# Two layers of a hybrid diffusion backbone in float32: moving query, key and norm jobs within the emission order

## The chip, the cores and the metric

One Trainium2 chip, one of its cores. The metric is the device time of one execution in microseconds. Three executions of the kernel before took 2201.49, 2202.52 and 2205.49 us; the median, 2202.52 us, is the time to be compared with. All tensors are float32.

## The reference, cut to what matters

A stream `x` of 512 latent tokens and a prefix of 256 context tokens go through two layers of width 1024. In the second layer (`last`) the context gives keys and values alone.

```python
for l in range(DEPTH):
    hx = modulate(x, norm1_g[l], sh1, sc1)          # RMSNorm, scale, shift
    hc = modulate(xc, norm1_g[l], csh1, csc1)
    ux = hx @ w_in[l]                               # one wide input projection
    uc = hc @ (w_in[l][:, :KV_COLS] if last else w_in[l])
    kv_c = kv_heads(uc[..., :KV_COLS], ...)         # keys, values of mixers B, C, D
    kv_x = kv_heads(ux[..., :KV_COLS], ..., rope)
    q_x = query_heads(ux, ..., rope)                # queries; D's latent queries cq = rms_norm(...)
    br_x = latent_branches(...)                     # A pooling, B 2-D neighbourhood,
                                                    # C windowed with sinks, D latent attention
    mixed_x = merge_branches(br_x, gate_logits, w_branch[l], w_out[l])
    ...
    x = x + g1 * mixed_x
    x = x + g2 * swiglu(modulate(x, norm2_g[l], sh2, sc2), ...)
return rms_norm(x, final_norm_g)
```

`merge_branches` sums over the four mixers `sigmoid(gate logits) * (y @ w_branch)`; each of the four gates is a projection of the normed stream to 1024 channels.

## The kernel before

**Arithmetic.** Everything lies feature-major: 128 features on the partitions, tokens on the free axis (768 = 512 latent, `PL`, and 256 context, `PC`; the second layer's queries and gates have `PL` only). A float32 product is made of three matmuls of rounded halves: `hi*hi + lo*hi + hi*lo` (`mm3`, L149 to L151). Each weight tile is loaded raw by a DMA that SyncE issues (L163), ScalarE rounds it to `hi` (L143), GpSimd subtracts for `lo` (L157; VectorE does it, L146, in a few places). A weight slab of 1024 x 128 comes as two halves of 256 KB; there are three raw buffers and four `hi`/`lo` buffers.

**Order of the work.** The program is written by a hand-made order of jobs, `Stream`. A job is a generator that emits matmuls and yields after some of them the TensorE time that they are reckoned to need. When a job is taken from the queue, its weights and those of the next job in the queue are loaded (`step`). `defer(us, fn)` emits `fn` once that much reckoned time has been emitted; `need(key)` emits it at once; `until(job)` emits jobs until that one is done and (if `late`) flushes the deferred ones. `drive(attend(heads))` alternates pieces of attention with steps of the waiting jobs, so that these jobs' matmuls fill TensorE while VectorE and ScalarE make the softmax. After that, the framework's scheduler lays each engine's instructions in a row, by priority of emission but with its own estimates of what is ready; only SyncE's order, that of the loads, is kept as written:

```python
ctx.enter_context(tc.manual_schedule(engines={SP}))
```

**PSUM.** Tags `mm` (3 banks, projections), `sc` (2, scores and the norm's `nh`), `tr` (2, transposes), `pv` (1). Scratch tiles of tag `t` (seven) hold rope halves, `tmv`, `krt`, `krx`, `braw` and others.

**Start of the second layer** (`mix`, L1325 to L1338). The pooling job runs (`ps_pool`), then the first neighbourhood queries (`ps_naq`), while the context's norm is finished: `norm.stats(PC)` and, 2.0 us of reckoned time later, `norm.apply(PC)` (L491 `ps_rstd`, L518 `nh`, L520 `hh`, L521 `hl`). Then come the token-major rows, `tm_jobs`: eight jobs with six accumulators (`ps_tm`), whose values are copied out (`tmv`, L665), stored to DRAM (`vst`, L667) and loaded back as values (`vraw`, L693 ff.). Then the first keys, `na_k_job(0)` (`ps_nak`, split by `split_k` into `k` tiles, L143, L146, L958), then attention B. `na_q_job(1)` (`ps_naq` again, weights `naqr`) and four gates of mixer A are the jobs that attention B is interleaved with. `na_bias` loads `braw` (L1004) and GpSimd adds the mask (L1011); these tables are needed by the first softmax (L1028).

**Mixer C in either layer** (L1358 to L1367). The keys job `swk` and the second queries job `swq` (both with rope: `rt` L143, then `rf` and `rt`, L1069, L1072, L1073, then the splits) run first; then attention C, interleaved with two `cq` jobs (the latent queries of D, with squares, statistics and a normalisation, `rms_jobs`) and six gates of mixer B. In attention, `sc` (L921, L922) are score matmuls, `mx` (L1108, L1110) maxima, `nm` their negative, `p` (L1114, L1115) the exponentials, normalised at L839, `tr` (L858) transposes, `pv` (L872) products with values.

**Norm behind a projection** (`project_jobs`). After each output tile `m` the residual `x` is made (`add_x`, L1458) and the tile's squares are deferred by 1.5 us (L1462; ScalarE L472 `nsq`, VectorE L473 `acc`). When the last of eight tiles is done, `stats` (L480 `ps_ssq`, then the small Newton steps `nwv`, `nwt`, then `dg`, L484) is deferred by 2.0 us and `apply` by 5.5 us.

Of the kernel before, what the change touches and what calls it, by code (L numbers as in the profile page):

```python
# [23 lines left out]
KD = D // 128  # L24
# [90 lines left out]
def kernel(ctx: ExitStack, tc: tile.TileContext, a: dict, out: bass.AP):  # L115
# [90 lines left out]
    def feat_job(w, c0, name, pieces, post):  # L206

        def run(ws):
            for p in pieces:
                ps = psum("mm", "ps_" + name, p[1] - p[0])  # L210
                yield from mm_piece(ps, ws, cur["h"], p)
                post(ps, p)
        return st.add(run, lambda: slab(w, c0, name))
# [413 lines left out]
    for l in range(2):  # L627
# [352 lines left out]
        def na_q_job(pr):  # L980
            q = []

            def post(ps, piece):
                if not q:
                    q.extend(new_q())
                split_q(ps, piece, q, True)
            return feat_job(w_in, O_NA_Q + 128 * pr, "naq", pieces, post), q

        def na_k_job(pr):
            k = []  # L990

            def post(ps, piece):
                if not k:
                    k.extend(new_k(4))
                split_k(ps, piece, k[0:2], k[2:4], True)
            return feat_job(w_in, O_NA_K + 128 * pr, "nak", (PL, PC), post), k
# [81 lines left out]
        def swa_q_job(g, tab):  # L1078
            q = []

            def post(src, piece):
                if not q:
                    q.extend(new_q())
                split_q(src, piece, q, False)
            return rope_job(O_SWA_Q + 128 * g, "swq", pieces, tab, post), q

        def swa_k_job(tab):
            k = []

            def post(src, piece):  # L1090
                if not k:
                    k.extend(new_k(4))
                split_k(src, piece, k[0:2], k[2:4], False)
            return rope_job(O_SWA_K, "swk", (PL, PC), tab, post), k
# [80 lines left out]
                    yield (s1 - s0) / 1200  # L1175
            return st.add(run)

        def rms_jobs(c0, dst, pieces_, name):

            box, acc_ = [], {}  # L1180

            def keep(i, ps, piece):
                if not box:
                    box.extend(dst())
                s0, s1 = piece
                n = s1 - s0
                hi, lo = (t[:, s0:s1] for t in box[i])
                act_copy(hi, ps)
                sub_hi(lo, ps, hi)
                if i == 0:  # L1190
                    acc_[piece] = tmp([128, n], F32, "nacc")
                acc = acc_[piece]
                square_add(acc, ps, i == 0)
                if i < len(box) - 1:
                    return

                def stats():
                    dg = rstd_diag(acc, n, 1.0 / (128 * len(box)))

                    def rest():  # L1200
                        rstd = rstd_rows(dg, n)
                        for j, b in enumerate(box):
                            hi, lo = (t[:, s0:s1] for t in b)
                            f = tmp([128, n], F32, "cf")
                            nc.vector.tensor_tensor(out=f, in0=hi.bitcast(F32), in1=lo.bitcast(F32), op=ALU.add)
                            nc.vector.scalar_tensor_tensor(out=f, in0=f, scalar=c_rms(l, len(box), j), in1=rstd, op0=ALU.mult, op1=ALU.mult)
                            act_copy(hi, f)
                            sub_hi(lo, f, hi)
                    st.defer(2.5, rest)
                st.defer(2.0, stats)  # L1210

            jobs = [feat_job(w_in, c0 + 128 * i, name, pieces_, lambda ps, p, i=i: keep(i, ps, p)) for i in range((1, 2)[name == "cq"])]
            return jobs[-1], box

        def mla_q_job(pr, tab, cq):
            qs = []
# [82 lines left out]
        def mix():  # L1299
            nam = big("c", [128, 3, 32, 8], F32, "nam")  # L1300
            nc.sync.dma_start(nam, a["k_namask"])
            y_pool = []
            bias, v = [], []

            def after_tm():
                v.extend((na_v(0, 4.0), na_v(1, 20.0)))
                rope_keys()
                cur["lo"] = nc.gpsimd

            if not last:  # L1310
                cur["lo"] = nc.vector

                tm = tm_jobs()
                for k in range(4):
                    ada_run((10, 10, 0, 0)[k])
                    st.until(tm[k], False)
                for k in range(4, KD):
                    start_h(k)
                jobs = pool_jobs(y_pool)
                jq0, q0 = na_q_job(0)  # L1320
                jk, k0 = na_k_job(0)
                st.until(tm[-1], False)
                after_tm()
                st.until(jobs[1], False)
            else:  # L1325
                jobs = pool_jobs(y_pool)
                jq0, q0 = na_q_job(0)
                norm.stats(PC)
                st.defer(2.0, lambda: norm.apply(PC), "norm")
                st.until(jobs[0], False)  # L1330
                st.need("norm")
                tm = tm_jobs()
                jk, k0 = na_k_job(0)
                st.until(tm[-1], False)
                after_tm()
            jq1, q1 = na_q_job(1)
            bias = [na_bias(e, nam) for e in range(2)]
            st.until(jk, False)  # L1338
            v0, v1 = v
            st.defer(24.0, lambda: bias.extend(na_bias(2 + e, nam) for e in range(2)), "bias")  # L1340
            y_na = [pair("y", TQ, "yn") for _ in range(2)]
            for m in range(4):
                g = gate_job(0, y_pool, m)
            st.drive(attend(na_heads(0, k0, q0, v0, bias[0:2], y_na[0])))
            jk, k1 = na_k_job(1)
            tab = [big("c", [128, 512], F32, "tab") for _ in range(2)]
            for i in range(2):
                nc.sync.dma_start(tab[i], a["k_rope"][:, i, :])
            vs = swa_v()
            g = gate_job(0, y_pool, 4)  # L1350
            st.until(g)
            st.need("bias")
            _, qs0 = swa_q_job(0, tab)
            jc, ck = rms_jobs(O_CKV, lambda: [pair("c", NT, "ck")], (PL, PC), "ckv")
            for m in range(5, KD):
                g = gate_job(0, y_pool, m)
            st.drive(attend(na_heads(1, k1, q1, v1, bias[2:4], y_na[1])))
            st.until(g)  # L1358
            jk, ks = swa_k_job(tab)
            jq, qs1 = swa_q_job(1, tab)  # L1360
            jc, cq = rms_jobs(O_CQ, lambda: [pair("c", TQ, "cq") for _ in range(2)], pieces, "cq")
            st.until(jq)
            y_swa = [pair("y", TQ, "ys") for _ in range(2)]
            for m in range(6):
                gate_job(1, y_na, m)
            heads = [h for g, q in enumerate((qs0, qs1)) for h in swa_heads(g, ks[g], ks[2 + g], q, vs, y_swa[g])]
            st.drive(attend(heads))  # L1367
            kt, vm = [], []
            rope_rows_job(kt)
            mtab = big("c", [128, 512], F32, "mtab")  # L1370
            nc.sync.dma_start(mtab, a["k_mrope"])
            mla_v_job(ck[0], vm)
            gate_job(1, y_na, 6)
            mla_k_job(0, ck[0], kt)
            _, qm = mla_q_job(0, mtab, cq)
            st.until(gate_job(1, y_na, 7))
            y_mla = [pair("y", TQ, "ym") for _ in range(2)]
            for m in range(4):
                gate_job(2, y_swa, m)
            st.drive(attend(mla_heads(qm, kt, vm[0:2], y_mla[0])))  # L1380
            mla_k_job(1, ck[0], kt)
            _, qm = mla_q_job(1, mtab, cq)
            st.until(gate_job(2, y_swa, 4))
            for m in range(5, KD):
                gate_job(2, y_swa, m)
            st.drive(attend(mla_heads(qm, kt, vm[2:4], y_mla[1])))
            return y_mla
# [61 lines left out]
        def project_jobs(w, name, h_, b, new_norm, first, rest, r0=0, kn=KD):  # L1449
# [4 lines left out]
            def add_x(ps, m, p):  # L1454
                s0, s1 = p
                c = 0 if s0 < NX else 1
                x = cur["x"][m][:, s0:s1]
                nc.vector.scalar_tensor_tensor(out=x, in0=ps, scalar=mods[l][:, b + m, c:c + 1], in1=x, op0=ALU.mult, op1=ALU.add)  # L1458
                if new_norm:
                    if not nm:  # L1460
                        nm[0] = new_norm()
                    st.defer(1.5, lambda: nm[0].squares(m, p), p)  # L1462

            def go(m, w_, ps_, tag="mm"):
                for p in ps_:
# [314 lines left out]
```

## Time and profile before

| | us |
|---|---|
| three executions | 2201.49, 2202.52, 2205.49 |
| the profiled execution, its own time | 2200.1 |
| its span, first to last instruction | 2198.3 |
| TensorE (PE) busy | 2131.2 (97% of the span) |
| VectorE (DVE) busy | 1261.2 (57%) |
| ScalarE (ACT) busy | 884.1 (40%) |
| GpSimd (POOL) busy | 732.7 (33%) |

The profiled execution took 2.42 us less than the median; 1.8 us of its 2200.1 lie outside the span. Busy times overlap; an engine's busy time is that of its instructions, without register, branch and semaphore work. A row of the timeline has the start in us from the span's start, the duration, the engine, the source line, the operation, what it writes and reads, the shape and, in brackets, the engine's idle time before it with what ended it. `SPq` and `ACTq` rows are the issuing of DMAs.

### The profile page before, as it was taken

Reading aid. Unit: us, or ns where it says so; the run is one execution under the profiler, and the core shown is the slowest. Engines: PE = TensorE matmul, PEld = TensorE weight load, DVE = VectorE, ACT = ScalarE, POOL = GpSimd, SP = SyncE. Lnnn points to the kernel's source line nnn. Section 1 sums busy time; section 2 is a strip of 40 time slices with the busy share of each in tenths; the row PEclk is TensorE's granted clock in tenths of the full one; section 3 lists DMA queues with packets and bytes.
Section 4 is the critical chain, followed back from the end, with each engine's and each line's share of the span. In section 5 each row is a group of like instructions: output and inputs, shape, how many; then the busy total and the mean of one; then the engine's idle time right before and its main releaser. Section 6 shows DMA issues by size and latency. Waiting matters only on the chain.

```text
span 2198.3 us, 32640 instructions
## 1 busy us (share of the span) xinstructions
PE 2131.2 (97%) x11840; PEld 1830.5 (83%) x11840; DVE 1261.2 (57%) x2818; ACT 884.1 (40%) x1981; POOL 732.7 (33%) x609
## 2 busy tenths in 40 slices
PE   6989999999999999999999999999999999999998
PEld 2878888888888888888888888887888898888886
DVE  6674667767789797554522255667777445212225
ACT  4364555544432322122212234556655434323233
POOL 1432222222232323323333333433333343444443
PEclk9999999999999999999999999999999999999999
DMA  7422121111455244444422232322222332333332
GB/s 239 114 61 62 48 51 44 39 49 49 127 175 151 85 150 133 143 140 149 151 75 63 70 111 83 103 66 66 56 65 70 88 115 82 96 96 97 103 93 91
DMA packets 317334, 211.59 MB, mean 96 GB/s; under 512 B 17371, under 2 KB 284917, under 8 KB 317173
## 3 DMA queue, kind: packets, MB, share of 16 engines
q1 hardware_dynamic: 308756, 201.65, 31.9%
q10 hardware_dynamic: 8416, 7.87, 1.1%
q8 instruction: 93, 1.52, 0.3%
q14 instruction: 69, 0.56, 0.1%
HBM read 202.90 MB, written 6.55 MB: 95 GB/s over the span
## 4 chain that ended last, share of the span: by engine, by line
PE 84%; DVE 6%; DMA 2%; ACT 2%; issue 2%; POOL 1%; ACTq 0%; SPq 0%; POOLq 0%; DVEq 0%
PE ps_w L149 13%; PE ps_w L150 13%; PE ps_w L151 13%; PE ps_gate L149 6%; PE ps_gate L150 6%; PE ps_gate L151 6%; PE pv L872 3%; PE tr L858 2%; PE ps_y L149 2%; PE ps_y L151 1%; PE ps_y L150 1%; PE ps_wo L151 1%; PE ps_wo L150 1%; PE ps_wo L149 1%; DMA wor<-in_w_out_dram 1%
## 5 line engine op out<-in xcount | busy, mean ns | idle before, releaser
L157 POOL TENSOR_TENSOR gatelo<-gater,gatehi 128x512 fp32r<-128x512 f32 x128 | 172.0, 1346 | 427.8 <-ACT gatehi L143 413.9
L149 PE MATMUL ps_gate<-hh,gatehi 128*128 128x512 f32 (+1 forms) x768 | 278.5, 363 | 1.2 <-ACT gt L807 1.2
L150 PE MATMUL ps_gate<-hl,gatehi 128*128 128x512 f32 (+1 forms) x768 | 273.5, 356 | 0.0
L151 PE MATMUL ps_gate<-hh,gatelo 128*128 128x512 f32 (+1 forms) x768 | 273.1, 356 | 0.0
L400 DVE SCALAR_TENSOR_TENSOR adaacc<-adaraw,cs,adaacc 128x512 f32<-128x512 f32 x224 | 160.8, 750 | 86.4 <-DMA adaraw<-in_ada_w_dram 85.1
L149 PE MATMUL ps_w<-hh,w1hi 128*128 128x512 f32 (+1 forms) x480 | 170.9, 356 | 0.0
L149 PE MATMUL ps_w<-hh,w3hi 128*128 128x512 f32 (+1 forms) x480 | 170.3, 355 | 0.0
L150 PE MATMUL ps_w<-hl,w1hi 128*128 128x512 f32 (+1 forms) x480 | 170.0, 354 | 0.0
L150 PE MATMUL ps_w<-hl,w3hi 128*128 128x512 f32 (+1 forms) x480 | 170.0, 354 | 0.0
L157 POOL TENSOR_TENSOR w1lo<-w1r,w1hi 128x512 fp32r<-128x512 f32 x80 | 103.6, 1296 | 198.9 <-ACT w1hi L143 196.9
L151 PE MATMUL ps_w<-hh,w1lo 128*128 128x512 f32 (+1 forms) x480 | 169.8, 354 | 0.0
L151 PE MATMUL ps_w<-hh,w3lo 128*128 128x512 f32 (+1 forms) x480 | 169.8, 354 | 0.0
L149 PE MATMUL ps_w<-gh,w2hi 128*128 128x512 f32 (+1 forms) x472 | 165.6, 351 | 0.0
L151 PE MATMUL ps_w<-gh,w2lo 128*128 128x512 f32 (+1 forms) x472 | 165.4, 350 | 0.0
L150 PE MATMUL ps_w<-gl,w2hi 128*128 128x512 f32 (+1 forms) x472 | 165.2, 350 | 0.0
L157 POOL TENSOR_TENSOR w3lo<-w3r,w3hi 128x512 fp32r<-128x512 f32 x80 | 105.5, 1325 | 178.1 <-ACT w3hi L143 170.3
L151 PEld LDWEIGHTS ps_gate<-hh,gatelo 128*128 128x128 f32 x768 | 145.1, 189 | 19.8
L149 PEld LDWEIGHTS ps_gate<-hh,gatehi 128*128 128x128 f32 x768 | 145.3, 189 | 19.0 <-ACT gt L807 1.4
L150 PEld LDWEIGHTS ps_gate<-hl,gatehi 128*128 128x128 f32 x768 | 145.4, 189 | 16.8
L157 POOL TENSOR_TENSOR w2lo<-w2r,w2hi 128x512 fp32r<-128x512 f32 (+1 forms) x80 | 97.4, 1224 | 158.2 <-ACT w2hi L143 156.9
L1515 DVE SCALAR_TENSOR_TENSOR ft<-ft,ps_w 128x512 f32<-128x512 f32 (+1 forms) x68 | 39.6, 582 | 143.9 <-ACT ft L1514 143.8
L143 ACT ACTIVATE gatehi<-gater 128x512 fp32r<-128x512 f32 x128 | 80.4, 630 | 83.4 <-PE ps_gate L150 41.9
(421 smaller groups left out, 5621.0 us busy)
## 6 DMA issues: line engine op xcount, KB each, us to landing
adaraw<-in_ada_w_dram SPq DMA_DIRECT2D x160, 256.0 KB
gater<-in_w_in_dram SPq DMA_DIRECT2D x128, 256.0 KB
w1r<-in_ffn_w_dram SPq DMA_DIRECT2D x80, 256.0 KB
w3r<-in_ffn_w_dram SPq DMA_DIRECT2D x80, 256.0 KB
w2r<-in_ffn_w_dram SPq DMA_DIRECT2D x56, 256.0 KB
ada<-in_ada_w_dram SPq DMA_DIRECT2D x32, 256.0 KB
wbr<-in_w_branch_dram SPq DMA_DIRECT2D x64, 128.0 KB
wor<-in_w_out_dram SPq DMA_DIRECT2D x32, 256.0 KB
```

Of the source, the lines that this page charges most:

```text
L143: nc.scalar.activation(out=o, in_=i, func=AF.Copy, scale=scale)
L149: nc.tensor.matmul(ps, ah, bh, start=start, stop=False)
L150: nc.tensor.matmul(ps, ah, bl, start=False, stop=False)
L151: return nc.tensor.matmul(ps, al, bh, start=False, stop=stop).ins
L157: cur["lo"].tensor_tensor(out=lo, in0=raw, in1=hi.bitcast(F32), op=ALU.subtract)
L400: nc.vector.scalar_tensor_tensor(out=acc[j], in0=raw, scalar=c, in1=acc[j], op0=ALU.mult, op1=ALU.add)
L858: nc.tensor.transpose(tr[:, 128 * j:128 * j + 128], ps[qi][0][:, c0:c0 + 128], ident)
L872: nc.tensor.matmul(acc[:, 128 * q0:128 * (q0 + nq)], v[rows], t[rows, c:c + 128 * nq], start=(i == 0), stop=(i == nmm - 1))
L1515: nc.vector.scalar_tensor_tensor(out=t, in0=t, scalar=1.0, in1=p1, op0=ALU.add, op1=ALU.mult)
```

## The change

Three edits. In mixer C, only the keys job precedes attention; the second queries and the two `cq` jobs follow in the queue, each with a gate before it: gate 0, `swq`, gate 1, `cq` 0, gate 2, `cq` 1, gates 3 to 5. In `add_x`, the last tile's squares are emitted at once, after any of the same piece that are still deferred. In the second layer, the job of the first keys stands ahead of the token-major rows, and `norm.apply(PC)` is deferred by 4.0 instead of 2.0 us.

```diff
-        def rms_jobs(c0, dst, pieces_, name):
+        def rms_jobs(c0, dst, pieces_, name, between=lambda i: None):
...
-            jobs = [feat_job(w_in, c0 + 128 * i, name, pieces_, lambda ps, p, i=i: keep(i, ps, p)) for i in range((1, 2)[name == "cq"])]
-            return jobs[-1], box
+            for i in range((1, 2)[name == "cq"]):
+                between(i)
+                job = feat_job(w_in, c0 + 128 * i, name, pieces_, lambda ps, p, i=i: keep(i, ps, p))
+            return job, box
...
                 jobs = pool_jobs(y_pool)
                 jq0, q0 = na_q_job(0)
+                jk, k0 = na_k_job(0)
                 norm.stats(PC)
-                st.defer(2.0, lambda: norm.apply(PC), "norm")
+                st.defer(4.0, lambda: norm.apply(PC), "norm")
                 st.until(jobs[0], False)
                 st.need("norm")
                 tm = tm_jobs()
-                jk, k0 = na_k_job(0)
                 st.until(tm[-1], False)
                 after_tm()
             jq1, q1 = na_q_job(1)
...
             jk, ks = swa_k_job(tab)
+            st.until(jk)
+            y_swa = [pair("y", TQ, "ys") for _ in range(2)]
+            gate_job(1, y_na, 0)
             jq, qs1 = swa_q_job(1, tab)
-            jc, cq = rms_jobs(O_CQ, lambda: [pair("c", TQ, "cq") for _ in range(2)], pieces, "cq")
-            st.until(jq)
-            y_swa = [pair("y", TQ, "ys") for _ in range(2)]
-            for m in range(6):
+            jc, cq = rms_jobs(O_CQ, lambda: [pair("c", TQ, "cq") for _ in range(2)], pieces, "cq", lambda i: gate_job(1, y_na, 1 + i))
+            for m in range(3, 6):
                 gate_job(1, y_na, m)
...
-                    st.defer(1.5, lambda: nm[0].squares(m, p), p)
+                    if m < KD - 1:
+                        st.defer(1.5, lambda: nm[0].squares(m, p), p)
+                    else:
+                        st.need(p)
+                        nm[0].squares(m, p)
```

## Rows read from the trace of the kernel before

**Rows 1.** The page: busy us of each engine, share of the span, instructions.
```profile
PE 2131.2 (97%) x11840; PEld 1830.5 (83%) x11840; DVE 1261.2 (57%) x2818; ACT 884.1 (40%) x1981; POOL 732.7 (33%) x609
```
**Rows 2.** PE's timeline in mixer C, rows with a wait (first, then second layer).
```profile
306.35 0.38 PE L921 MATMUL sc<-k,q 128*128 128x256 f32 x1 [1.90 <-DVE mx L1108]
...
339.41 0.70 PE L491 MATMUL ps_rstd<-dg,ones 128*128 128x256 f32 x2 [1.02 <-DVE dg L484]
...
1505.15 0.38 PE L921 MATMUL sc<-k,q 128*128 128x256 f32 x1 [1.13 <-ACT p L1114]
...
1511.79 0.39 PE L921 MATMUL sc<-k,q 128*128 128x256 f32 x1 [2.36 <-DVE mx L1108]
...
1532.77 0.30 PE L858 MATMUL tr<-ident,p 128*128 128x128 f32 x1 [0.69 <-DVE pl L146]
```
**Rows 3.** Timeline around the second layer's keys of mixer C: PE, DVE, POOL.
```profile
1494.70 0.28 PE L151 MATMUL ps_swk<-hh,swklo 128*128 128x256 f32 x1
...
1495.28 3.44 POOL L157 TENSOR_TENSOR cqlo<-cqr,cqhi 128x512 fp32r<-128x512 f32 x2 [8.12 <-ACT cqhi L143]
...
1495.90 1.66 DVE L1073 TENSOR_TENSOR rf<-rf,rt 128x512 f32<-128x512 f32 x1
...
1499.62 0.42 DVE L958 CAST k<-k 64x512 fp32r<-64x512 f32 x1
...
1506.00 0.68 DVE L1073 TENSOR_TENSOR rf<-rf,rt 128x512 f32<-128x512 f32 x1
```
**Rows 4.** Timeline at the first layer's last `wo` tile: squares, statistics, norm.
```profile
737.01 0.75 DVE L1458 SCALAR_TENSOR_TENSOR x<-ps_wo,mod,x 128x512 f32<-128x512 f32 x1 [3.48 <-PE ps_wo L151]
737.79 0.63 ACT L472 ACTIVATE nsq<-x 128x512 f32<-128x512 f32 x1 [4.99 <-DVE x L1458]
...
738.46 0.69 DVE L473 TENSOR_TENSOR acc<-acc,nsq 128x512 f32<-128x512 f32 x1 [0.70 <-ACT nsq L472]
...
739.68 0.95 PE L480 MATMUL ps_ssq<-ones,acc 128*128 128x2 f32 x8
```
**Rows 5.** PE's timeline at the second layer's start, rows that matter.
```profile
1327.11 0.70 PE L491 MATMUL ps_rstd<-dg,ones 128*128 128x256 f32 x2 [0.92 <-DVE pb L727]
...
1337.21 0.46 PE L149 MATMUL ps_tm<-tmhi,hh 128*128 128x416 f32 x1 [1.23 <-DVE hl L521]
...
1358.94 0.39 PE L149 MATMUL ps_nak<-hh,nakhi 128*128 128x512 f32 x1
...
1367.30 0.25 PE L921 MATMUL sc<-k,q 128*128 128x192 f32 x1
...
1370.02 0.50 PE L151 MATMUL ps_naq<-hh,naqlo 128*128 128x512 f32 x1 [0.81 <-POOL naqlo L157]
...
1378.16 0.33 PE L858 MATMUL tr<-ident,p 128*128 128x128 f32 x1 [1.75 <-DVE p L839]
...
1380.30 0.52 PE L858 MATMUL tr<-ident,p 128*128 128x128 f32 x3 [0.88 <-DVE p L839]
```
**Rows 6.** The loads and weight splits there: SyncE's issues, ACT, POOL.
```profile
1360.23 1.98 SPq L1004 DMA_DIRECT2D braw<-in_k_rpb_dram  x2
1363.93 2.44 SPq L163 DMA_DIRECT2D naqr<-in_w_in_dram  x2
...
1367.81 0.63 ACT L143 ACTIVATE naqhi<-naqr 128x512 fp32r<-128x512 f32 x1 [0.33 <-DMA naqr<-in_w_in_dram]
...
1368.52 1.45 POOL L157 TENSOR_TENSOR naqlo<-naqr,naqhi 128x512 fp32r<-128x512 f32 x1 [0.32 <-ACT naqhi L143]
1370.59 1.30 POOL L157 TENSOR_TENSOR naqlo<-naqr,naqhi 128x512 fp32r<-128x512 f32 x1 [0.62 <-DMA gater<-in_w_in_dram]
```
**Rows 7.** SyncE's own waits, 1320 to 1400 us: total us, times, longest us.
```profile
SPq L1004 <- DMA vst<-tmv: 9.4, 2, 8.6
```
**Rows 8.** PE's timeline where it stood longest after the start-up.
```profile
124.98 0.56 PE L149 MATMUL ps_pw<-yph,pwh 128*128 128x256 f32 x1 [4.69 <-DVE ypl L766]
```
**Rows 9.** Stretch behind that: us, busy PE, PEld, DVE, ACT, POOL, PEclk, DMA, GB/s.
```profile
125.10:128.40 3.30, 3.22 (x10) 2.31 (x11) 3.03 (x6) 3.18 (x8) 2.68 (x2) 0.50 0.18 36
```

## The prediction

> **What bounds the kernel now.** I read the page's busy times first [rows 1]: TensorE (PE) is busy for 97% of the span, VectorE for 57%. The change adds and removes no matmul, so the time can move only through the moments in which PE stands. Next I took PE's waits by releaser, and then its timeline at the places that the change touches. There the reader is to look at the brackets: how long PE stood, and for whom.
>
> In mixer C it stands five times that matter [rows 2]: 1.90 us in the first layer and 1.13 and 2.36 us in the second, all in the first 17 us of attention C and for the softmax; later 1.02 us for the statistics of the latent queries and 0.69 us for a transposed tile. At the second layer's start it stands 0.92 us for the context's norm, 1.23 us for its last halves, 0.81 us for weights, and 1.75 and 0.88 us for the first softmax [rows 5]. That is 7.10 + 5.59 = 12.69 us, 0.6% of the time: at these places no more can be won.
>
> **Part 1, last squares at once: 0.** This edit changes priority alone. In the trace the deferred squares are not late: the residual ends at 737.76, ScalarE squares it from 737.79, VectorE has added it by 739.15, and the statistics' matmuls start at 739.68 [rows 4]. They stand behind two steps of other matmuls in the program (2.0 us of deferral), which the edit leaves alone. The three norms that have such a tile show the same pattern. What hides the squares is an idle ScalarE; without that, one square and one addition (0.63 + 0.69 us) would wait. I take 0, with 0.5 us either way.
>
> **Part 2, mixer C: -2.6.** Moved are the `swq` job (24 matmuls a piece, two weight loads, four copies on ScalarE, three rope steps and the splits on VectorE), the two `cq` jobs with their two loads each, and three gates with three loads each. SyncE has the gate's three loads ahead of `swq`'s; all find their buffers as the old ones did, since each job takes two of the same four halves. GpSimd has the same number of differences in another order.
>
> What goes: the three early waits, 1.90 + 1.13 + 2.36 = 5.39 us, in which the softmax stood behind the rope of `swq`, now two jobs later. What stays: 1.02 + 0.69, whose chains are only moved. What is new: the keys were covered by `swq`. The last key matmul starts at 1494.70 and the last copy of the first head's keys ends at 1500.04 [rows 3], 5.2 us later once that matmul is through. The gate that now follows in the queue is ready and would fill PE, if the framework's scheduler puts it ahead of the scores; it does order by its estimates: ScalarE had rounded `cqhi` by 1495.28, ahead of its copies of the older keys, whose rope was not added until 1495.90 [rows 3]. If the scores stand first, every gate matmul waits behind them on PE, and the softmax with them. So the wait is between 0 and 5.2 us in either layer. It hangs on how far the scheduler's estimate is off, and the rope's last addition took 1.66 us beside GpSimd's `cqlo` and 0.68 us at another moment [rows 3]: about 1 us of surprise. I take 0.7 us in either layer, 1.4, nearest to that row.
>
> The Trainium skill (SBUF — State Buffer, section "Who interferes with whom") says that a VectorE instruction with two inputs in SBUF and a GpSimd one that reads SBUF shut each other out for a whole instruction. By that rule the longer of the two durations holds wherever a weight split falls on the keys, and without it the sum would be 1.4 us lower; the 1.66 us agree with the rule.
>
> The moved rope also meets a running softmax later; I take the same 0.7 us for it in each layer, 1.4. Sum: -5.39 + 1.4 + 1.4 = -2.6 us. Bounds: -7.1 (all five waits go, none comes) and +5.0 (the scores wait 5.2 us in both layers: 10.4 - 5.4).
>
> **Part 3, the first keys ahead of the rows: +4.1.** Moved are 48 matmuls, two loads and the splits of the keys. They ran from 1358.94 to 1367.30 [rows 5], 8.36 us, which is 36 matmuls of 512 columns at 0.232 us. In that time something else went on. SyncE waited up to 8.6 us for the stores of the rows before it could load the bias tables [rows 7], at 1360.23; the second queries' weights stand behind these in its queue, with the first gates' behind them, and were issued from 1363.93 on [rows 6]. ScalarE rounded the first half at 1367.81, GpSimd was through with it at 1368.52 + 1.45 = 1369.97 and with the second at 1371.89. PE, with 8.36 us of keys to do, still stood 0.81 us for them.
>
> This order of loads is unchanged, since SyncE's is kept as written and `na_q_job(1)` is loaded only when `drive` takes it. Counted from the end of the rows, the halves arrive at +11.03 and +12.95 us. Before, the keys and 10.86 us of other things lay between the rows and the first transposes (1378.16 - 1367.30); of these 0.81 + 1.75 were waits, 8.30 work. After the change PE has about 1.2 us of scores, then nothing until the first half is there; 10 matmuls take it to 13.35, 12 more to 16.1, and up to 1.2 us of scores and transposes to 17.3. Against 10.86 that is 5.2 to 6.4 us later; I take 6.0, since waits rarely pack. Off go the 0.88 us of the second transposes, whose softmax starts earlier now, and 1.0 of the norm's 0.92 + 1.23: the keys give the context's norm 5 us more, but their own accumulators hold banks that the rows need. Sum: 6.0 - 0.9 - 1.0 = +4.1 us. Bounds: -5.6 (all five waits go, none comes) and +8.1 (6.4 us and nothing saved, and 1.7 us of half clock, below).
>
> **Sum.** 0 - 2.6 + 4.1 = +1.5 us on the profiled execution's 2200.1, so 2201.6; that execution lies 2.4 us under the median, so 2204.0 us is to be compared with 2202.52. A measurement of this kernel can tell 0.2%, 4.4 us, from no change.
>
> **Rivals.**
>
> *Rival 1, slower: the gap also costs the clock.* After the longest stand, 4.69 us [rows 8], TensorE was granted 0.50 of its clock (1.2 of 2.4 GHz) from 125.1 to 128.4 us [rows 9]: 3.3 us of work done in half, 1.7 us lost. A gap of 8 us at the second layer's start would be followed by the same, so part 3 costs 6.4 + 1.7 = 8.1 us with no norm wait saved; with part 2 at -2.6 that is +5.5, 2208.0. It decides as soon as part 3 costs over 7.0. For it: the load order; against: the matmuls that follow wait for a second half anyway, so half a clock hides there. On the page TensorE: Matmul & The Clock Gate (section "What's actually happening") the Trainium skill calls the half rate the default that activity lifts; by that rule this gap is followed by it, and rows 8 and 9 agree.
>
> *Rival 2, faster: the weights are not late.* If the store that SyncE waits for lands sooner, or the scheduler keeps some of the rows' matmuls for the gap, part 3 is at its lower bound: -5.6 - 2.6 = -8.2, 2194.3. For it: the loads' issue has only 1.3 us after the rows to wait for stores [rows 5, 6]. Against: all of the chain behind it is measured, and 36 matmuls of cover are gone.
>
> *Rival 3, part 2 does nothing.* The scheduler orders by its own estimates already, and waits only change place: 0 + 4.1, 2206.6, inside 0.2%. For it: the same estimates made the old waits; against: the rope itself leaves the busiest stretch.
>
> **How the numbers follow.** Forecast 0.42, rival 1 0.30, rival 2 0.20, rival 3 0.08. The forecast's own spread puts 0.02 of it beyond 0.2% on each side. Faster is then 0.20 + 0.02 = 0.22, slower 0.30 + 0.02 = 0.32, same 0.38 + 0.08 = 0.46. As cases of both signs hold half of the chance, the forecast's own range is 2200 to 2207.5. The range of 8 in 10 goes from 2196.5 to 2210.5: it leaves out half of rival 2 (0.10) and the upper end of rival 1, with part 2 near its upper bound (0.08).
>
> **What would show it.** Part 1 is right if `ps_ssq` follows its last square as before and no wait of a norm goes. Part 2 is right if no wait over 1 us stands in the first 17 us of attention C, and a new one of under 1.5 us stands at the first scores. Part 3 is right if, after the last `ps_tm`, PE stands some 8 us in all for `naqhi` and `naqlo`, with `braw` still ahead of them on SyncE, and no longer stands for the first softmax. It is wrong if these weights are ready within 3 us of the rows' end; the sum is wrong too if waits arise away from these places, since the scheduler lays the whole program anew.

## The result and the profile after

The kernel after takes 2217.22 us (median of six executions, 2211.88 to 2220.01); the kernel before took 2203.17 beside it (six executions, 2200.33 to 2205.49). The ratio is 1.0065, with a 95% interval of 1.0051 to 1.0079: slower by 14 us, where +1.5 was forecast and 2210.5 was the upper end of the range. The profiled execution of the kernel after is one of its longer ones (2218.24 us, span 2216.4), that of the kernel before one of its shorter ones, so between the spans of these two traces 18.1 us are to be found.

The page's first part, to be held against [rows 1]:

```profile
PE 2138.9 (97%) x11840; PEld 1834.3 (83%) x11840; DVE 1260.0 (57%) x2818; ACT 884.4 (40%) x1981; POOL 730.7 (33%) x609
```

The work is the same, instruction for instruction. PE's busy time is 7.7 us longer for the same 11840 matmuls, and the rest of the 18.1 us is standing. To find where, I cut both traces at the same PE instructions. The views below have a row for each of three stretches: from the first layer's last key matmul of mixer C to its first `wo` matmul; from the last pooling matmul to the second layer's first key matmul of mixer C; from its last key matmul to its first `wo` matmul. The columns are those of [rows 9], with the stretch's length after its bounds. First the kernel before:

```profile
290.88:679.25 388.37, 380.74 (x2349) 336.05 (x2347) 300.70 (x709) 191.55 (x503) 94.98 (x83) 1.00 0.29 81
1322.63:1486.51 163.88, 156.72 (x829) 134.38 (x828) 98.21 (x276) 89.53 (x206) 61.71 (x56) 1.00 0.32 86
1494.70:1767.75 273.05, 265.36 (x1369) 218.31 (x1368) 186.65 (x440) 151.80 (x386) 96.42 (x85) 1.00 0.28 72
```

Then the kernel after:

```profile
291.04:690.07 399.03, 385.72 (x2349) 338.52 (x2348) 300.29 (x709) 192.35 (x502) 94.18 (x82) 0.99 0.28 78
1334.13:1502.77 168.64, 158.87 (x829) 135.90 (x828) 97.45 (x276) 88.41 (x207) 61.05 (x57) 0.97 0.31 83
1510.96:1787.46 276.50, 266.59 (x1370) 219.24 (x1369) 185.10 (x440) 151.88 (x385) 95.42 (x84) 0.99 0.27 70
```

The lengths differ by +10.66, +4.76 and +3.45 us, 18.87 in all; the other stretches give 0.8 back. So the first layer's mixer C, where no loss was expected, holds more than half. PE's timeline there, rows with large brackets that the kernel before does not have:

```profile
295.28 0.50 PE L921 MATMUL sc<-k,q 128*128 128x256 f32 x2 [1.21 <-ACT k L143]
...
299.26 0.44 PE L921 MATMUL sc<-k,q 128*128 128x384 f32 x1 [0.62 <-DVE mx L1108]
...
306.93 0.85 PE L858 MATMUL tr<-ident,p 128*128 128x128 f32 x6 [0.83 <-DVE nm L831]
...
330.55 0.90 PE L858 MATMUL tr<-ident,p 128*128 128x128 f32 x3 [1.64 <-DVE p L839]
...
377.07 1.05 PE L480 MATMUL ps_ssq<-ones,nacc 128*128 128x2 f32 x8 [2.87 <-DVE nacc L473]
...
396.59 0.38 PE L921 MATMUL sc<-k,q 128*128 128x256 f32 x1 [0.67 <-DVE cf L1206]
...
451.30 0.47 PE L149 MATMUL ps_uq<-cqh,wqhi 128*128 128x512 f32 x1 [1.72 <-DVE qt L1233]
```

In the first 17 us of attention C stands what was forecast: no 1.90 us wait of the softmax any more, and a new one of 1.21 us at the first scores. The loss lies behind it: 1.64 us for a normalised tile, 2.87 us for the latent queries' sum of squares, and 1.72 us in mixer D, where 1.23 us stood at a neighbouring matmul before (`wqlo`, 436.00). Behind the first two of these the granted clock is half. The same view by stretches, of the kernel after, with the second layer's start and mixer D's start in the second layer as third and fourth row:

```profile
330.50:333.90 3.40, 3.35 (x10) 2.66 (x11) 2.26 (x7) 1.75 (x5) 0.00 (x0) 0.50 0.00 0
378.30:381.70 3.40, 3.40 (x11) 2.72 (x10) 2.88 (x16) 2.00 (x7) 0.00 (x0) 0.50 0.20 68
1381.80:1392.00 10.20, 5.20 (x11) 3.68 (x12) 5.09 (x14) 3.50 (x11) 8.06 (x9) 0.50 0.65 176
1634.40:1637.80 3.40, 3.40 (x10) 2.62 (x9) 1.99 (x6) 1.24 (x4) 0.99 (x1) 0.50 0.30 77
```

Taking half of PE's busy time in such a stretch as lost, an estimate from these rows gives 1.7, 1.7, 2.6 and 1.7 us. (One and the same place, shown in the last section, has 21 matmuls in 3.40 us at the full clock and 11 at half.) At the second layer's start, the loads, the rounding and PE, to be held against [rows 5, 6]:

```profile
1377.70 0.35 PE L151 MATMUL ps_tm<-tmhi,hl 128*128 128x416 f32 x1
...
1379.22 1.42 SPq L1004 DMA_DIRECT2D braw<-in_k_rpb_dram  x2
1380.74 1.27 SPq L163 DMA_DIRECT2D naqr<-in_w_in_dram  x2
...
1385.29 0.63 ACT L143 ACTIVATE naqhi<-naqr 128x512 fp32r<-128x512 f32 x1 [5.76 <-POOL bias L1011]
...
1385.97 0.80 PE L149 MATMUL ps_naq<-hh,naqhi 128*128 128x512 f32 x1 [6.59 <-ACT naqhi L143]
...
1388.03 0.80 PE L151 MATMUL ps_naq<-hh,naqlo 128*128 128x512 f32 x1 [0.83 <-POOL naqlo L157]
```

`braw` is still ahead of `naqr` on SyncE, and PE stands 7.42 us for the two halves. (The row of `naqhi` names GpSimd's bias tables; in the kernel with all parts and both repairs the same row names the load, `[5.99 <-DMA naqr<-in_w_in_dram]`.) SyncE itself waited up to 14.1 us for the rows' stores ahead of `braw`, where [rows 7] have 8.6 (here from 1340 to 1410 us):

```profile
SPq L1004 <- DMA vst<-tmv: 14.4, 2, 14.1
```

In the second layer's mixer C the two waits of [rows 2] are gone and others have come, the longest far behind, at the scores of mixer D:

```profile
1515.20 0.50 PE L921 MATMUL sc<-k,q 128*128 128x256 f32 x2 [1.21 <-ACT k L143]
...
1632.74 0.50 PE L149 MATMUL sc<-k,q 96*128 96x512 f32 x1 [2.76 <-ACT p L1283]
```

### The profile page after: what moved, and what is told of

It reads as the page before. It is cut to its first block, busy times and chain, and to the rows that moved or that the text cites. A ratio compares the mean times of both kernels' runs of the same rounds, so it can differ in the third digit from the quotient of the medians.

```text
span 2216.4 us, 32641 instructions
## 1 busy us (share of the span) xinstructions
PE 2138.9 (97%) x11840; PEld 1834.3 (83%) x11840; DVE 1260.0 (57%) x2818; ACT 884.4 (40%) x1981; POOL 730.7 (33%) x609
## 5 line engine op out<-in xcount | busy, mean ns | idle before, releaser
L157 POOL TENSOR_TENSOR w3lo<-w3r,w3hi 128x512 fp32r<-128x512 f32 x80 | 105.1, 1320 | 179.1 <-ACT w3hi L143 177.6
L149 PEld LDWEIGHTS ps_gate<-hh,gatehi 128*128 128x128 f32 x768 | 145.9, 190 | 19.2 <-ACT gt L807 1.4
```

What stands on the lines that cost most here:

```text
L149: nc.tensor.matmul(ps, ah, bh, start=start, stop=False)
L157: cur["lo"].tensor_tensor(out=lo, in0=raw, in1=hi.bitcast(F32), op=ALU.subtract)
```

## The experiments

**The parts one by one.** The first three kernels are the kernel before with one part of the change each; their diffs are parts of the one shown above (the edit in `add_x`; those in `rms_jobs` and mixer C; the one in the second layer's start).

> Part 1 alone: the last tile's squares at once, all else as before. Theory (the loss of 14 us sits in mixer C of the first layer, and part 1 is worth nothing): within 2 us of the kernel before, and the statistics' matmuls of the norms start as in rows 4. Rival A (the framework's scheduler lays the whole program anew at any edit, and this alone moves the time): 5 us or more away in either direction, with waits at places that no edit touches.

Measured: 2200.87 us against 2201.79, ratio 1.0004 (0.9996 to 1.0013). The theory's figure holds. In its trace the last square starts at 738.75 and the statistics' matmuls at 740.64, 1.89 us apart as in [rows 4].

> Part 2 alone: in mixer C only the keys precede attention, the second queries and the latent queries stand between gates, in both layers. Theory (the normalisation of the latent queries now meets a running softmax on VectorE, and the waits that follow lower the granted clock): +8 to +14 us, with the 2.87 us wait for the latent queries' sum of squares and the stretches at 0.50 of the clock in the first layer's mixer C, as in the trace of the kernel after. Rival A (part 2 is worth its forecast, the 14 us come from part 3 and from where its waits fall in the clock): -5 to +2 us. Rival B (the parts are not additive: either alone is harmless): within 2 us.

Measured: 2211.95 us against 2201.79, ratio 1.0053 (1.0039 to 1.0066), some 12 us. The theory holds: 2.88 us for the sum of squares and half clock are there again.

> Part 3 alone: the second layer's first keys precede its token-major rows, the context's norm is deferred by 4.0 instead of 2.0 us. Theory (the second queries' weights come late, behind the bias tables on SyncE): +3 to +7 us, with some 7 us of standing for the two halves of these weights and a stretch at 0.50 of the clock behind it. Rival A (most of the 14 us is here): +10 us or more. Rival C (the weights are late only after part 2's delay): -5 to 0 us.

Measured: 2206.02 us, ratio 1.0024 (1.0015 to 1.0034), some 5 us. PE stands 6.69 and 0.84 us for the two halves, and 0.50 of the clock stands behind it. The three parts add up: 0.0004 + 0.0053 + 0.0024 = 0.0081, against 0.0065 for the whole; the intervals overlap.

**Part 3 with its loads in order.** Part 3 alone, with this edit on top:

```diff
                 tm = tm_jobs()
+                jq1, q1 = na_q_job(1)
                 st.until(tm[-1], False)
                 after_tm()
-            jq1, q1 = na_q_job(1)
+            if not last:
+                jq1, q1 = na_q_job(1)
```

> Part 3 with its load order mended: in the second layer the job of the second queries is queued right behind the rows' jobs, so that SyncE issues its weights ahead of the stores' wait and the bias tables. Theory (the loss of part 3 is this load order alone): the 7 us of standing for the weights go, no stretch at half clock at the second layer's start, and the time is 0 to 6 us below the kernel before. Rival D (the gap stays, and only its name changes, since attention B's first softmax waits for the bias tables in the same queue, which are then later by two loads): +2 to +7 us, with PE standing for the first transposes instead.

Measured: 2204.48 us, ratio 1.0016 (1.0005 to 1.0027). My theory falls, rival D's figure holds. SyncE now issues `naqr` at 1355.82 and PE no longer stands for it, but the next weights in the same queue, and then the values, which ScalarE loads, are late instead. PE's timeline:

```profile
1378.65 0.50 PE L149 MATMUL ps_gate<-hh,gatehi 128*128 128x512 f32 x1 [2.20 <-ACT gatehi L143]
...
1381.00 0.50 PE L151 MATMUL ps_gate<-hh,gatelo 128*128 128x512 f32 x1 [1.16 <-POOL gatelo L157]
...
1391.53 0.39 PE L872 MATMUL pv<-ph,v 128*128 128x256 f32 x1 [1.60 <-DVE v L146]
```

So it is not the place of one pair of loads alone. It fits these rows that the keys' 8.36 us were the cover for all that is stored and loaded between the rows and attention B, since the gates and the values now come late one after the other; no run tests this by itself. Whether anything is gained over part 3 alone (1.0024) the intervals cannot tell.

**Part 2 taken apart.** From the kernel before; the first diff is mixer C with only the second queries moved, the second with only the latent queries taken apart (both with `between` in `rms_jobs` where it is used).

```diff
+            st.until(jk)
+            y_swa = [pair("y", TQ, "ys") for _ in range(2)]
+            gate_job(1, y_na, 0)
             jq, qs1 = swa_q_job(1, tab)
             jc, cq = rms_jobs(O_CQ, lambda: [pair("c", TQ, "cq") for _ in range(2)], pieces, "cq")
-            st.until(jq)
-            y_swa = [pair("y", TQ, "ys") for _ in range(2)]
-            for m in range(6):
+            for m in range(1, 6):
```

> From the kernel before: in mixer C of both layers only the second queries move (keys, attention begins, gate 0, second queries); the two latent-query jobs stay unbroken behind them, then gates 1 to 5. Theory (the loss of part 2 is the latent queries' sum of squares, which now stands among gates whose weights GpSimd splits; the second queries' move costs little): -2 to +4 us. Rival A (the moved rope of the second queries and the keys' lost cover are the loss): +7 to +12 us, the same as part 2 alone.

Measured: 2207.08 us against 2202.26, ratio 1.0024 (1.0014 to 1.0034), 5 us: between the theory's figure and the rival's. The 1.64 us wait at the normalised tile is here too, behind the second queries' rope and splits on VectorE. Its VectorE and PE rows:

```profile
322.63 1.58 DVE L1073 TENSOR_TENSOR rf<-rf,rt 128x512 f32<-128x512 f32 x1
...
324.92 1.71 DVE L971 SCALAR_TENSOR_TENSOR q<-rf,q 64x512 fp32r<-64x512 f32 x2
...
327.42 0.15 DVE L831 TENSOR_SCALAR nm<-mx 128x1 f32<-128x1 f32 x1
...
330.70 0.48 DVE L839 TENSOR_SCALAR p<-p,rs 128x512 f32<-128x512 f32 x1
...
331.24 0.72 PE L858 MATMUL tr<-ident,p 128*128 128x128 f32 x3 [1.64 <-DVE p L839]
```

```diff
             jq, qs1 = swa_q_job(1, tab)
-            jc, cq = rms_jobs(O_CQ, lambda: [pair("c", TQ, "cq") for _ in range(2)], pieces, "cq")
             st.until(jq)
             y_swa = [pair("y", TQ, "ys") for _ in range(2)]
-            for m in range(6):
+            jc, cq = rms_jobs(O_CQ, lambda: [pair("c", TQ, "cq") for _ in range(2)], pieces, "cq", lambda i: gate_job(1, y_na, i))
+            for m in range(2, 6):
```

> From the kernel before: the second queries stay ahead of attention C, only the latent queries are taken apart (gate 0, latent 0, gate 1, latent 1, gates 2 to 5). Theory (the latent queries' chain among the gates is the loss): +4 to +9 us, with a wait of some 3 us for their sum of squares and half clock behind it in the first layer. Rival A (the second queries' move is the loss): -2 to +2 us.

Measured: 2205.28 us, ratio 1.0012 (1.0000 to 1.0024), 2.6 us, between the two figures; the interval reaches both. The theory's wait does not come: taken apart by themselves, the latent queries show no wait for the sum of squares. The waits of [rows 2] for the maxima are still there (1.89 and 2.33 us), since the second queries are still in front. By the middles of the ratios the two halves of part 2 cost 8 us by themselves and 12 together, so some of the loss may be what they do to each other; the intervals are too wide to settle that.

Next, part 2 in the first layer alone (`if not last:` around the new lines, the old ones behind `else:`).

> Part 2 in the first layer alone. Theory (in the trace the first layer's mixer C holds +9.5 us and the second layer's +2 to +3): +7 to +11 us. Rival (the layers share the loss, and the profiled execution was not typical): +4 to +6 us.

Measured: 2211.43 us, ratio 1.0038 (1.0024 to 1.0051), 8 us. The theory's figure holds, though the interval (5.3 to 11.2 us) touches the rival's.

**The sum of squares.** Around the wait of 2.87 us the kernel after shows, on GpSimd and VectorE:

```profile
373.62 2.85 POOL L157 TENSOR_TENSOR gatelo<-gater,gatehi 128x512 fp32r<-128x512 f32 x2 [6.56 <-ACT gatehi L143]
...
373.85 1.50 DVE L146 TENSOR_TENSOR ysl<-yf,ysh 128x256 fp32r<-128x256 f32 x1
...
375.27 1.74 DVE L473 TENSOR_TENSOR nacc<-nacc,nsq 128x512 f32<-128x512 f32 x1
```

The addition `nacc` took 0.68 us in the kernel before. The view of this tile has minimum, median and maximum of its three additions in ns, in the kernel before and then after:

```profile
L473 DVE TENSOR_TENSOR nacc<-nacc,nsq x3: 416/676/691, 322.6 to 1520.9; 128x512 f32<-128x512 f32 x2, 128x256 f32<-128x256 f32 x1
```

```profile
L473 DVE TENSOR_TENSOR nacc<-nacc,nsq x3: 416/691/1744, 375.3 to 1568.3; 128x512 f32<-128x512 f32 x2, 128x256 f32<-128x256 f32 x1
```

Both VectorE instructions have two inputs in SBUF, and each ends a little after one of GpSimd's two splits (the second at 373.62 + 2.85 = 376.47, `nacc` at 375.27 + 1.74 = 377.01). This agrees with the rule of the Trainium skill (SBUF — State Buffer, section "Who interferes with whom") that the prediction weighed for the keys alone. The addition alone takes 0.69 us and the copy 0.42 us (medians of the kernel after), so the two are some 2.1 us longer here, most of the 2.87.

That a gate follows the latent queries is not enough for this. In the kernel before and in the one with only the latent queries taken apart, a split meets this addition too, but starts after it, and the addition takes 0.68 us; in the two kernels of part 2 below with a gate ahead of the scores no split meets it (0.69 us). In the kernel after the second split had started 0.25 us ahead of the addition. So it counts which of the two begins first, and that moved with part 2. The next kernel is part 2 with the statistics emitted later:

```diff
-                st.defer(2.0, stats)
+                st.defer(4.5 if name == "cq" else 2.0, stats)
```

> Part 2 with the latent queries' statistics deferred by 4.5 instead of 2.0 us of reckoned time. Theory (the sum of squares is late because the addition on VectorE and a copy ahead of it last 1.74 and 1.50 us beside GpSimd's split of gate weights, and PE stands behind it): the 2.88 us wait goes, the half clock behind it too, and the time is 3 to 6 us below part 2 alone. Rival (the wait only comes later in the same chain, at its diagonal or at the scores): within 2 us of part 2 alone.

Measured: 2207.47 us, ratio 1.0029 (1.0016 to 1.0041), against 1.0053 for part 2 alone: some 5 us less. The theory holds; the wait and the half clock at that place are gone, and transposes wait 0.86 and 0.72 us there. The addition is as long as before, so the deferral takes away PE's wait for it and not its cause:

```profile
376.69 1.78 DVE L473 TENSOR_TENSOR nacc<-nacc,nsq 128x512 f32<-128x512 f32 x1
```

**The cover of attention's start.** Two kernels emit gate 0 ahead of the first scores instead of among them: one in the order of the kernel before, one in part 2 with late statistics.

```diff
             jq, qs1 = swa_q_job(1, tab)
-            jc, cq = rms_jobs(O_CQ, lambda: [pair("c", TQ, "cq") for _ in range(2)], pieces, "cq")
             st.until(jq)
             y_swa = [pair("y", TQ, "ys") for _ in range(2)]
-            for m in range(6):
+            g = gate_job(1, y_na, 0)
+            jc, cq = rms_jobs(O_CQ, lambda: [pair("c", TQ, "cq") for _ in range(2)], pieces, "cq")
+            st.until(g)
+            for m in range(1, 6):
```

> From the kernel before: keys, second queries, then the first gate of mixer B, and only then attention C begins; all else of mixer C stays (latent queries first, then gates 1 to 5). Theory (the waits of 1.90, 1.13 and 2.36 us in rows 2 are the rope of the second queries in front of the softmax, and one gate of matmuls before the first scores covers it): these three go and none over 1 us takes their place in the first 17 us of attention C, so -2 to -5 us. Rival (one gate fewer among the attention tiles is missed later, or the waits only change place): -1 to +3 us.

Measured: 2199.88 us against 2202.86, ratio 0.9987 (0.9976 to 0.9997), -3 us, as the theory has it, but by another way: in the first layer the 1.90 us wait is gone and the stretch of mixer C 4.9 us shorter (waits of 1.23 and 1.21 us at 436 and 600 us are gone too; the second is also absent with part 3 alone, which leaves mixer C as it was), in the second layer waits have changed place, as the rival has it:

```profile
1510.01 0.45 PE L921 MATMUL sc<-k,q 128*128 128x384 f32 x1 [0.78 <-DVE mx L1108]
...
1512.85 0.39 PE L921 MATMUL sc<-k,q 128*128 128x256 f32 x1 [2.22 <-ACT p L1114]
```

For part 2 the edit is this, beside the late statistics:

```diff
             st.until(jk)
             y_swa = [pair("y", TQ, "ys") for _ in range(2)]
-            gate_job(1, y_na, 0)
+            g = gate_job(1, y_na, 0)
             jq, qs1 = swa_q_job(1, tab)
             jc, cq = rms_jobs(O_CQ, lambda: [pair("c", TQ, "cq") for _ in range(2)], pieces, "cq", lambda i: gate_job(1, y_na, 1 + i))
+            st.until(g)
             for m in range(3, 6):
```

> Part 2 with two repairs: the latent queries' statistics deferred by 4.5 us of reckoned time, and gate 0 emitted ahead of the first scores, so that the keys are covered. Theory (the loss of part 2 is a sum of separate waits; the scores' 1.21 and 0.27 us in either layer go, the sum of squares' 2.88 us is gone already, and the rope of the second queries in the running softmax stays): +1 to +5 us against the kernel before, 1 to 4 us below part 2 with late statistics alone. Rival (waits fall anew wherever attention runs short of cover, so a repair of one is paid by another): within 1.5 us of part 2 with late statistics alone, at +5 to +8 us.

Measured: 2198.11 us (2194.63 to 2201.89), ratio 0.9981 (0.9971 to 0.9991): 4 us faster than the kernel before, some 10 us below part 2 with late statistics by the two ratios. One gate does more than either theory gave it, and this kernel beats both kernels of the case. Its three stretches, to be held against those of the kernel before, and all that is left of long waits in the first layer's mixer C up to 400 us:

```profile
289.73:676.68 386.95, 381.04 (x2349) 335.89 (x2347) 299.47 (x709) 192.04 (x503) 94.70 (x82) 1.00 0.29 81
1319.39:1483.82 164.43, 156.63 (x829) 134.35 (x828) 98.66 (x276) 89.81 (x207) 62.30 (x57) 1.00 0.33 86
1492.02:1763.76 271.74, 265.81 (x1369) 218.58 (x1368) 185.26 (x440) 152.71 (x385) 94.90 (x84) 1.00 0.28 72
```

```profile
313.68 0.33 PE L858 MATMUL tr<-ident,p 128*128 128x128 f32 x1 [1.26 <-DVE pl L146]
...
378.11 0.67 PE L491 MATMUL ps_rstd<-dg,ones 128*128 128x256 f32 x2 [1.10 <-DVE dg L484]
```

Mixer C is 1.42 us shorter than before in the first layer and 1.31 us in the second. The first figure may be no more than scatter: with part 3 alone, whose mixer C is that of the kernel before, the same stretch took 386.86 us. In the second layer one wait of 1.64 us stands at the scores (1504.34). The first scores no longer wait for keys, and the wait of 1.64 us behind the second queries' rope is gone too, though the rope still meets a running softmax; 1.26 us for `pl` stand in its place.

**Which of the two repairs.** The same without the late statistics, and then all three parts of the change with both repairs:

> Part 2 with one repair alone: gate 0 emitted ahead of the first scores, the statistics deferred by 2.0 us as in the change. Theory (most of part 2's loss is that attention C begins on uncovered keys, and all that follows then falls out of step with its cover): -4 to 0 us against the kernel before, within 3 us of the kernel with both repairs. Rival (the sum of squares that waits for VectorE is a loss of its own, and the deferral is needed for the gain): +1 to +5 us, with the wait of some 2.9 us for it still there.

Measured: 2200.18 us against 2200.78, ratio 0.9996 (0.9983 to 1.0008). The theory's first figure holds, and one gate ahead of the scores takes back nearly all that part 2 lost (12.5 us by the two ratios). The late statistics would be worth some 3 us more (0.9981 against 0.9996), but the intervals overlap. In kind the rival is right as well: without them PE stands for the latent queries' diagonal, and the clock is at half for part of the next 5 us:

```profile
380.96 0.70 PE L491 MATMUL ps_rstd<-dg,ones 128*128 128x256 f32 x2 [2.47 <-DVE dg L484]
```

```profile
381.50:386.50 5.00, 5.00 (x23) 4.51 (x22) 4.48 (x13) 1.14 (x3) 0.73 (x1) 0.66 0.35 88
```

> The kernel after, with part 2's two repairs (gate 0 ahead of the first scores, statistics at 4.5 us); parts 1 and 3 as in the change. Theory (the parts add: part 1 nothing, repaired part 2 -4, part 3 +4): within 3 us of the kernel before, 12 to 17 us below the kernel after, with the 6.6 us wait for the second queries' weights still there. Rival (the parts act on each other through the clock): +6 us or more, or a gain of over 4 us.

Measured: 2203.88 us against 2200.78, ratio 1.0011 (1.0000 to 1.0022), 2.4 us over the kernel before by the ratio, and 12 us below the kernel after by the two ratios (1.0065 - 1.0011), the lower end of the theory's figure. The theory holds; the wait for the second queries' weights is 6.83 us. So two edits in mixer C take back some 12 of the change's 14 us. The 2.4 us left agree, within the intervals, with part 3's 5 less the 4 that the repaired mixer C gains.

## Why the prediction was wrong

**The failed step is part 2's sum, "-5.39 + 1.4 + 1.4 = -2.6 us", and its upper bound of +5.0.** By itself the part cost some 12 us. Its first term was right: the waits at the start went. The second was 1.6 us too low: the scores wait 1.21 + 0.28 us in each layer, where 0.7 stood in the sum.

The third term, 0.7 us a layer for the moved rope, was mis-sized: 1.64 + 0.35 us of standing and 1.7 us of half clock in the first layer. And a term was missing. "What stays: 1.02 + 0.69, whose chains are only moved" took the latent queries' statistics as unchanged; moved together with the second queries, with GpSimd's splits on top of their addition, they cost 2.87 + 0.60 + 0.67 us and 1.7 us of half clock. The upper bound looked at the first scores alone; it had to take in every chain that is moved into a running softmax, with the clock behind each. Together, the first layer's waits up to 400 us (9.25 us where the kernel before had 3.30) and the half clock (3.4 by the estimate) account for 9.4 of the 10.66 us.

In the second layer waits grew even outside attention C: 2.76 us at mixer D's scores, where 0.63 us stood in the kernel before. All kernels that moved the second queries without a gate ahead of the scores show it (2.67, 2.72 and 2.66 us in the three with that order in both layers), the repaired ones do not (0.65 us). That one gate takes away waits 35 to 120 us further on is shown; by which steps it does so was not tried.

**Part 3 was right in the wait that it named; its size came near in part by luck.** Forecast +4.1 with bounds up to +8.1, measured some 5 us (3.3 to 7.5 by the interval). Of the stretch's 4.76 us only 2.6 are added standing, less than forecast; `naqr` was issued some 2.7 us behind the rows' end and not 5.0. The other 2.15 us are PE's longer busy time, which the forecast left to rival 1. PE stands 7.42 us for the halves where "some 8 us in all" was said, `braw` is ahead of them, the first softmax's 1.75 and 0.88 us are gone. Rival 1's mechanism came too: 0.50 of the clock for 10.2 us, in which 5.20 us of work cost 2.6 us. Of the norm's waits the 1.23 us went and the 0.92 us stayed.

**Part 1 was right**: nothing that its interval (-0.9 to +2.9 us) can tell from 0.

**The rivals.** None had the result. Rival 1 named the half clock at one place; it came there and at three more. Rival 2's "weights are not late" is refuted by 6.59 us; the repaired loads show that even then no gain is left, because the loads behind them are next. Rival 3's "waits only change place" is what happened in part 2, but the new places were worse.

## What to carry over

When a job is moved from ahead of an interleaved stage into it, cost each of its chains on the shared engines at its new place, not only the wait that it leaves behind; and add a half clock behind each new wait as a possible cost (1.7 us at three of the four places here). Ask what covers the first operands of the stage: here one gate of ready matmuls ahead of the first scores was worth 10 to 12.5 us in one order and 3 in another. What looks like a wait for one load may be missing cover for many.

## What was not expected of the hardware

Whether the clock falls behind a wait cannot be read from the wait's length, nor from its place. With part 1 alone mixer C is that of the kernel before, and the first softmax's wait is the same, 1.89 us at 306.81 against 1.90 at 306.35. Behind it the clock was full in the one profiled execution and at half in the other. First the kernel before, then part 1 alone:

```profile
306.40:309.80 3.40, 3.40 (x21) 2.98 (x22) 2.60 (x11) 3.00 (x11) 0.63 (x1) 1.00 0.32 77
```

```profile
306.90:310.30 3.40, 3.40 (x11) 2.82 (x12) 1.57 (x6) 2.73 (x11) 0.60 (x1) 0.51 0.32 77
```

So too the 1.64 us wait of part 2: in the kernel with part 2 in the first layer alone it stands at 329.30, and the clock stays full:

```profile
329.30:332.70 3.40, 3.40 (x23) 3.10 (x24) 3.30 (x9) 1.94 (x7) 0.00 (x0) 1.00 0.00 0
```

In the kernel after the same wait was followed by 0.50, while the longer ones of 2.36 us in [rows 2] and 2.22 us with the gate ahead of attention were not. The stretches behind these two, of the kernel before and of that kernel:

```profile
1511.80:1515.20 3.40, 3.40 (x16) 2.83 (x17) 2.25 (x9) 2.65 (x10) 0.00 (x0) 1.00 0.10 29
```

```profile
1512.90:1516.30 3.40, 3.40 (x16) 2.74 (x16) 2.20 (x6) 1.65 (x7) 1.55 (x2) 1.00 0.35 77
```

Within one kernel the time goes with the clock. Over the 103 executions of the kernel before that ran beside the experiments (2194.28 to 2209.07 us), time and mean granted clock have a correlation of -0.84. Taking time x (1 - mean clock) as what the clock costs, it is 14.1 us in the mean for the kernel before, 19.2 for the kernel after and 11.2 for the repaired mixer C. By this estimate some 5 of the change's 14 us and some 3 of the repair's 4 are clock, and the rest is standing. It counts half of all time at half clock, also where PE stands (5.1 us for the stretch at 1381.80, of which 2.6 by its busy time), so it is an upper figure.
